# A decoder block on one core: the first MLP matrix multiplied with 512 columns instead of twice 256

## The chip, the cores and the metric

The kernel runs on one core of a Trainium2 chip. The metric is the device time of one execution in microseconds (us). Before the change three runs took 435.99, 436.06 and 436.56 us; their median is 436.06 us.

## The reference: what is computed

One decoder block for 256 tokens of width 1024, in float32: a gated mixer and block attention in parallel, an output projection, a squared-ReLU MLP, a gated embedding and a final norm. The change is in the MLP's first matrix:

```
x = x + merged @ w_out
h = rms_norm(x, norm_ffn_g)
x = x + square(relu(h @ w_ff1)) @ w_ff2      # w_ff1: 1024 x 4096, w_ff2: 4096 x 1024
```

The kernel multiplies the gained x without its norm factor and multiplies the squared result by the factor's square at the end.

## The kernel before

Each float32 operand of a matrix product is split into two parts that TensorE multiplies in one pass each: the high part (a rounded copy, made on ScalarE) and the low part (the rest, a subtraction on VectorE). A product is then the sum of three: high weights by high x, high weights by low x, low weights by high x. `mm3` (L116 to L119) issues these three for a block of 128 weight columns: 128 rows of weights against 256 columns (tokens).

Weights come as tiles of 1 MB in the order in which they are used (L34 to L45). A tile's load needs one of four raw buffers, its split (two pieces, each one ScalarE copy at L84 and one VectorE subtraction at L85) one of three pairs of split buffers. `weights` (L95) issues, on the engines' in-order queues, the splits up to two tiles ahead of the tile that it returns.

The MLP has 16 tiles of `w_ff1` and 16 of `w_ff2`. A tile of `w_ff1` gives 256 of the 4096 hidden features as two blocks f of 128 features, and each block takes eight steps k over the 1024 inputs: 16 triples of matmuls. Hidden features come in four groups b of four tiles j. The order on TensorE is: tiles (b=0, j=0) and (0,1) together (L556), which close 6 of 8 steps of all four blocks first and then the last two steps; tile (0,2); 16 transposes that bring x into token order (L584); tile (0,3); then tile (1,0), the first tile of `w_ff2` (24 matmuls of 512 columns, L125 to L128), tile (1,1), the next of `w_ff2`, and so on alternating.

A tile's result lies in one bank of PSUM, both blocks side by side (2 x 256 columns). Three banks rotate under the tag `mm` (L133); a matmul that starts a bank waits until the bank's last reader is done. After each tile `ff1_post` (L543) reads the bank once with a relu on ScalarE (L551), squares on VectorE (L553) and splits the square on ScalarE and VectorE (L107, L108). After tile (0,2) VectorE also copies the 16 transposes (L585, four copies), ScalarE squares them (L586, two), and the split of the first `w_ff2` tile stands behind these squares in ScalarE's queue; behind that stands the relu of tile (0,3).

Of the kernel before, what the change touches and what calls it, by code (L numbers as in the profile page):

```python
# [10 lines left out]
F32 = mybir.dt.float32  # L11
F32R = mybir.dt.float32r
AF = mybir.ActivationFunctionType
OP = mybir.AluOpType
AX = mybir.AxisListType

P = 128
S = 256
D = 1024
KD = D // P  # L20
# [3 lines left out]
CW = 256  # L24
# [26 lines left out]
def block_kernel(ctx: ExitStack, tc: tile.TileContext, xt, xk, pt, rows, wst, bsp, rel, buckets, wts, out):  # L51
    nc = tc.nc
    const = ctx.enter_context(tc.tile_pool(name="const", bufs=1))
    act = ctx.enter_context(tc.tile_pool(name="act", bufs=1))
    wpool = ctx.enter_context(tc.tile_pool(name="wpool", bufs=1))
    tmp = ctx.enter_context(tc.tile_pool(name="tmp", bufs=2))
# [30 lines left out]
    def split_to(n):  # L87
        while state["split"] < min(n, NTILE):
            i = state["split"]
            load_to(i + 4)  # L90
            split_tiles(i)
            for s in (slice(0, 1024), slice(1024, 2048)):
                split_piece(i, s)

    def weights(key, width, ahead=3):  # L95
        i = POS[key]
        split_to(i + ahead)
        k = 2048 // width
        return (hi[i].rearrange("p (k c) -> p k c", k=k), lo[i].rearrange("p (k c) -> p k c", k=k))


    def pair_tile(tag, name, k=KD):
        return act.tile([P, k, 2, S], F32R, tag=tag, name=name)

    def split_act(dst, src):

        nc.scalar.activation(dst[:, :, 0], src, AF.Copy)  # L107
        nc.vector.tensor_sub(dst[:, :, 1], src, dst[:, :, 0].bitcast(F32))  # L108
# [7 lines left out]
    def mm3(o, wh, wl, x, first, last, **kw):  # L116
        nc.tensor.matmul(o, wh, x[:, 0], start=first, stop=False, **kw)  # L117
        nc.tensor.matmul(o, wh, x[:, 1], start=False, stop=False, **kw)  # L118
        nc.tensor.matmul(o, wl, x[:, 0], start=False, stop=last, **kw)  # L119
# [13 lines left out]
    def bank(tag="mm", bufs=3, shape=(P, 2, 256)):  # L133
        return ps.tile(list(shape), F32, tag=tag, name=f"{tag}_t", bufs=bufs)
# [80 lines left out]
    def proj_T(key, x, mid=None, ahead=3):  # L215

        wh, wl = weights(key, CW, ahead)
        o = bank()
        for f in range(2):
            fs = slice(f * P, (f + 1) * P)  # L220
            for k in range(KD):
                mm3(o[:, f], wh[:, k, fs], wl[:, k, fs], x[:, k], k == 0, k == KD - 1)
            if f == 0 and mid:
                mid()
        return o
# [49 lines left out]


    sgu_a = act.tile([P, 2, D], F32, tag="kT", name="sgu_a")
    sgu_b = act.tile([P, 2, D], F32, tag="ln", name="sgu_b")
    wsT = sgu_a[:, 0].rearrange("p (g t) -> p g t", g=8)
    bsg = sgu_a[:, 1].rearrange("p (g t) -> p g t", g=8)  # L280
    ln_g, ln_b = sgu_b[:, 0], sgu_b[:, 1]

    def row_bcast(eng, dst, src):
        eng.dma_start(dst, bass.AP(tensor=src.tensor, offset=src.offset, ap=[[0, P], [1, D]]))
# [42 lines left out]
    o = proj_T(("w_in", 0), xg2)  # L327
# [4 lines left out]
    o = proj_T(("w_in", 1), xg2)  # L332
# [3 lines left out]
    o = proj_T(("w_in", 2), xg2)  # L336
    u_post(2, o)
    normalise_x(3)
    o = proj_T(("w_in", 3), xg2)
# [37 lines left out]
    for j in range(4):  # L377
        o = proj_T(("w_in", 8 + j), hT)
# [11 lines left out]
    sc_sb, pt_sb, yb = {}, {}, {}  # L390
# [91 lines left out]
    for J in range(2):  # L482
        a, b, c = 2 * J, 2 * J + 1, 4 * J
# [19 lines left out]
    xs1 = pair_tile("xA", "xs1")  # L503
# [10 lines left out]
    for i in range(3):  # L514
        wh, wl = weights(("w_out", i), 1024)
# [10 lines left out]
    wh, wl = weights(("w_out", 3), 1024, ahead=2)  # L526
# [13 lines left out]

    fs_ = {}

    def ff1_post(b, j, o):  # L543
        if j == 0:
            if b % 2 == 0:
                f8 = pair_tile("xB", f"fs{b}")
                fs_[b] = [f8[:, :4], f8[:, 4:]]
            else:
                fs_[b] = [pair_tile(tag, f"fs{b}{tag}", 4) for tag in ("qT", "kT")]
        r = tmp.tile([P, 2, S], F32, tag="th", name=f"r{b}_{j}", bufs=3)  # L550
        nc.scalar.activation(r, o, AF.Relu)  # L551
        q2 = tmp.tile([P, 2, S], F32, tag="sq", name=f"q{b}_{j}")
        nc.vector.tensor_mul(q2, r, r)  # L553
        split_act(fs_[b][j // 2][:, 2 * (j % 2):2 * (j % 2) + 2], q2)

    def ff1_pair():  # L556

        ws = [weights(("w_ff1", j), CW, ahead=3 - j) for j in range(2)]
        os_ = [bank(), bank()]
        for ks in (range(6), range(6, KD)):  # L560
            for j, (wh, wl) in enumerate(ws):
                for f in range(2):
                    fs = slice(f * P, (f + 1) * P)
                    for k in ks:
                        mm3(os_[j][:, f], wh[:, k, fs], wl[:, k, fs], xs1[:, k],
                            k == 0 and f == 0, k == KD - 1, skip_group_check=True)
        return os_


    late = act.tile([P, 4, D], F32, tag="TB", name="late")  # L570
# [7 lines left out]
    def x1_by_token():  # L578

        for t in range(2):  # L580
            for a in range(2):
                tb = ps_acc.tile([P, 512], F32, tag=f"acc{2 * t + a}", name=f"x1t{t}{a}")
                for k in range(4):
                    nc.tensor.transpose(tb[:, k * P:(k + 1) * P], xT[:, 4 * a + k, t * P:(t + 1) * P], ident)  # L584
                nc.vector.tensor_copy(x2[:, t, halves(a)], tb)  # L585
            nc.scalar.activation(scratch, x2[:, t], AF.Square, accum_out=ssq[:, 0, t:t + 1])  # L586
        m = small.tile([P, 2], F32, tag="ms", name="ms_x1")
        nc.vector.tensor_scalar(m, ssq[:, 0], 1.0 / D, EPS, op0=OP.mult, op1=OP.add)
        r = small.tile([P, 2], F32, tag="rr", name="rr_x1", bufs=1)
        nc.vector.reciprocal(r, m)  # L590
        return r

    for j, o in enumerate(ff1_pair()):
        ff1_post(0, j, o)
    ff1_post(0, 2, proj_T(("w_ff1", 2), xs1))
    rr1 = x1_by_token()
    ff1_post(0, 3, proj_T(("w_ff1", 3), xs1))
    row_bcast(nc.gpsimd, gfin, rows[2])
    nc.gpsimd.dma_start(pT, pt)
    split_act(pTs, pT)  # L600
# [3 lines left out]
    def ff2(b, j):  # L604
        wh, wl = weights(("w_ff2", 4 * b + j), 1024)
        for k in range(2):
            kk = 2 * j + k
            for c in range(2):
                tok3(acc[c], fs_[b][kk // 4][:, kk % 4], wh[:, k, halves(c)], wl[:, k, halves(c)],
                     b == 0 and kk == 0, False)  # L610

    for b in range(1, 4):
        for j in range(4):
            ff1_post(b, j, proj_T(("w_ff1", 4 * b + j), xs1))
            ff2(b - 1, j)
    for j in range(3):
        ff2(3, j)
# [58 lines left out]
    for i in range(2):  # L676
        wh, wl = weights(("w_ple_gate", i), 1024, ahead=3 - i)
# [136 lines left out]
```

## Time and profile before

| | |
|---|---|
| median of three runs | 436.06 us |
| the profiled execution | 436.34 us, of which the span of the trace is 434.5 us |
| TensorE busy | 424.8 us (98%) |
| VectorE busy | 268.7 us (62%) |
| ScalarE busy | 225.2 us (52%) |

The trace is of one execution. What lies outside the span is 1.84 us. In the rows further down, PE is TensorE, DVE is VectorE, ACT is ScalarE; times are from the start of the span. Matmuls are pipelined: the duration in a row is from the start of one to its end, while the next starts earlier; how fast the engine goes is read from the distance of the starts.

### The profile page before, as it was taken

Reading aid. Unit: us, or ns where it says so; the run is one execution under the profiler, and the core shown is the slowest. Engines: PE = TensorE matmul, PEld = TensorE weight load, DVE = VectorE, ACT = ScalarE, POOL = GpSimd, SP = SyncE. Lnnn points to the kernel's source line nnn. Section 1 sums busy time; section 2 is a strip of 40 time slices with the busy share of each in tenths; the row PEclk is TensorE's granted clock in tenths of the full one; section 3 lists DMA queues with packets and bytes.
Section 4 is the critical chain, followed back from the end, with each engine's and each line's share of the span. In section 5 each row is a group of like instructions: output and inputs, shape, how many; then the busy total and the mean of one; then the engine's idle time right before and its main releaser. Section 6 shows DMA issues by size and latency. Waiting matters only on the chain.

```text
span 434.5 us, 6951 instructions
## 1 busy us (share of the span) xinstructions
PE 424.8 (98%) x2908; PEld 389.5 (90%) x2908; DVE 268.7 (62%) x359; ACT 225.2 (52%) x351; POOL 13.0 (3%) x21
## 2 busy tenths in 40 slices
PE   8999999999999999999999999999999999999992
PEld 7789999988999989999999999999999999888882
DVE  3676889576765657745558765555555555546544
ACT  5685544266573656554355764444444444434824
POOL 1001020000000000000000000000000000000012
PEclk9999999999999999999999999999999999999997
DMA  8999549533525525455254475554555554552002
GB/s 271 424 385 380 191 160 388 212 117 134 202 66 181 194 99 195 145 195 195 97 195 151 164 288 198 193 193 186 179 185 179 171 189 181 190 198 89 2 2 97
DMA packets 13407, 81.02 MB, mean 186 GB/s; under 512 B 1509, under 2 KB 1781, under 8 KB 4800
## 3 DMA queue, kind: packets, MB, share of 16 engines
q1 hardware_dynamic: 12240, 77.34, 48.8%
q0 software_dynamic: 848, 2.96, 1.9%
q8 instruction: 23, 0.38, 0.4%
q10 hardware_dynamic: 288, 0.27, 0.2%
q14 instruction: 8, 0.07, 0.0%
HBM read 79.49 MB, written 1.07 MB: 185 GB/s over the span
## 4 chain that ended last, share of the span: by engine, by line
PE 90%; DMA 4%; ACT 2%; DVE 1%; issue 1%; POOL 0%; SPq 0%; POOLq 0%; ACTq 0%
PE mm_t L117 17%; PE mm_t L118 16%; PE mm_t L119 16%; PE y L125 7%; PE y L128 7%; PE y L127 7%; DMA raw<-wts 4%; PE acc L117 2%; PE mm_t L125 2%; PE acc L118 2%; PE acc L119 2%; PE mm_t L127 2%; PE mm_t L128 2%; PE mm_t L431 1%; PE sp L397 1%; PE yb_t L442 1%
## 5 line engine op out<-in xcount | busy, mean ns | idle before, releaser
L85 DVE TENSOR_TENSOR lo<-raw,hi 128x1024 fp32r<-128x1024 f32 (+1 forms) x140 | 162.7, 1206 | 62.0 <-ACT hi L84 62.0
L84 ACT ACTIVATE hi<-raw 128x1024 fp32r<-128x1024 f32 (+1 forms) x140 | 138.0, 1036 | 37.6 <-issue 25.1
L117 PE MATMUL mm_t<-hT,hi 128*128 128x256 f32 x256 | 74.4, 291 | 0.0
L117 PE MATMUL mm_t<-xs,hi 128*128 128x256 f32 x256 | 72.5, 283 | 0.0
L119 PE MATMUL mm_t<-xs,lo 128*128 128x256 f32 x256 | 72.4, 283 | 0.0
L118 PE MATMUL mm_t<-xs,hi 128*128 128x256 f32 x256 | 72.4, 283 | 0.0
L118 PE MATMUL mm_t<-hT,hi 128*128 128x256 f32 x256 | 72.3, 283 | 0.0
L119 PE MATMUL mm_t<-hT,lo 128*128 128x256 f32 x256 | 72.3, 283 | 0.0
L117 PEld LDWEIGHTS mm_t<-hT,hi 128*128 128x128 f32 x256 | 48.9, 191 | 2.6 <-issue 1.2
L118 PEld LDWEIGHTS mm_t<-xs,hi 128*128 128x128 f32 x256 | 49.1, 192 | 0.4
L117 PEld LDWEIGHTS mm_t<-xs,hi 128*128 128x128 f32 x256 | 49.1, 192 | 0.4
L119 PEld LDWEIGHTS mm_t<-xs,lo 128*128 128x128 f32 x256 | 49.1, 192 | 0.0
L118 PEld LDWEIGHTS mm_t<-hT,hi 128*128 128x128 f32 x256 | 49.0, 191 | 0.1
L119 PEld LDWEIGHTS mm_t<-hT,lo 128*128 128x128 f32 x256 | 48.9, 191 | 0.0
L551 ACT ACTIVATE r<-mm_t 128x512 f32<-128x512 f32 x16 | 9.5, 593 | 44.5 <-PE mm_t L119 44.5
L553 DVE TENSOR_TENSOR q<-r 128x512 f32<-128x512 f32 x16 | 11.0, 690 | 34.0 <-ACT r L551 34.0
L412 ACT ACTIVATE s<-s,nm 128x256 f32<-128x256 f32 (+1 forms) x32 | 14.2, 444 | 22.8 <-DVE nm L408 22.8
L128 PE MATMUL y<-hi,fs 128*128 128x512 f32 x64 | 24.9, 390 | 0.0
L127 PE MATMUL y<-lo,fs 128*128 128x512 f32 x64 | 24.9, 390 | 0.0
L125 PE MATMUL y<-hi,fs 128*128 128x512 f32 x64 | 19.8, 391 | 0.0
L117 PE MATMUL acc<-mT,hi 128*128 128x256 f32 x64 | 18.2, 285 | 0.0
L117 PE MATMUL mm_t<-xg,hi 128*128 128x256 f32 x64 | 18.2, 284 | 0.0
(195 smaller groups left out, 728.1 us busy)
## 6 DMA issues: line engine op xcount, KB each, us to landing
raw<-wts SPq DMA_DIRECT2D x67, 1024.0 KB, 4.9
TB<-rvd POOLq DMA_DIRECT2D x1, 2048.0 KB, 15.6
raw<-wts SPq DMA_DIRECT2D x4, 256.0 KB, 4.7
raw<-wts SPq DMA_DIRECT2D x2, 512.0 KB, 6.8
xtok<-xk SPq DMA_DIRECT2D x2, 512.0 KB, 10.3
sgu_b<-rows SPq DMA_DIRECT2D x2, 512.0 KB, 9.9
out<-ots SPq DMA_DIRECT2D x4, 256.0 KB, 2.0
xg<-xt SPq DMA_DIRECT2D x1, 512.0 KB, 7.4
```

The costliest lines, as they stand in the source:

```text
L84: nc.scalar.activation(hi[i][:, s], raw[i][:, s], AF.Copy)
L85: nc.vector.tensor_tensor(lo[i][:, s], raw[i][:, s], hi[i].bitcast(F32)[:, s], op=OP.subtract)
L117: nc.tensor.matmul(o, wh, x[:, 0], start=first, stop=False, **kw)
L118: nc.tensor.matmul(o, wh, x[:, 1], start=False, stop=False, **kw)
L119: nc.tensor.matmul(o, wl, x[:, 0], start=False, stop=last, **kw)
L125: nc.tensor.matmul(os_[t], x[:, 0, ts[t]], wh, start=first, stop=False)
L127: nc.tensor.matmul(os_[t], x[:, 0, ts[t]], wl, start=False, stop=False)
L128: nc.tensor.matmul(os_[t], x[:, 1, ts[t]], wh, start=False, stop=last)
L397: nc.tensor.matmul(sp[:, h, 0:256], qT[rs, c, P:2 * P], kT_[0][rs, c], start=True, stop=True)
L412: nc.scalar.activation(s[:, h, cs], s[:, h, cs], AF.Exp, bias=nm[:, i, h:h + 1], accum_out=sm[:, i, h:h + 1])
L551: nc.scalar.activation(r, o, AF.Relu)
L553: nc.vector.tensor_mul(q2, r, r)
```

## The change

The high weights are multiplied by both parts of x in one matmul of 512 columns (the high part's 256 and the low part's 256 lie side by side), so that a triple becomes a pair: one matmul of 512 columns that fills a whole bank, and one of 256 columns (low weights by high x) that adds to the bank's first half. The two halves of the bank have to be added. Each block f of a tile now has a bank of its own, two for a tile; ScalarE copies each to SBUF, VectorE adds the halves of both blocks (one operation), and one further VectorE operation does relu and square. The first two tiles use all three `mm` banks and the bank `yb`. The copies go to a buffer in the place of the two layer norm rows, which is cut in two.

```diff
-    sgu_b = act.tile([P, 2, D], F32, tag="ln", name="sgu_b")
+    ln_g, ln_b = [act.tile([P, D], F32, tag="ln", name=n, bufs=2) for n in ("ln_g", "ln_b")]
...
-    def ff1_post(b, j, o):
+    def ff1_mm(o, wh, wl, f, k):
+
+        fs = slice(f * P, (f + 1) * P)
+        nc.tensor.matmul(o, wh[:, k, fs], xs1[:, k], start=k == 0, stop=False, skip_group_check=True)
+        nc.tensor.matmul(o[:, 0], wl[:, k, fs], xs1[:, k, 0], start=False, stop=k == KD - 1, skip_group_check=True)
+
+    def ff1_copy(z, f, o):
+        nc.scalar.activation(z[:, f], o, AF.Copy)
+
+    def ff1_z(b, j):
+        return act.tile([P, 2, 2, S], F32, tag="ln", name=f"z{b}_{j}", bufs=2)
+
+    def ff1_tile(b, j):
+        wh, wl = weights(("w_ff1", 4 * b + j), CW)
+        z = ff1_z(b, j)
+        for f in range(2):
+            o = bank()
+            for k in range(KD):
+                ff1_mm(o, wh, wl, f, k)
+            ff1_copy(z, f, o)
+        ff1_post(b, j, z)
+
+    def ff1_post(b, j, z):
...
-        r = tmp.tile([P, 2, S], F32, tag="th", name=f"r{b}_{j}", bufs=3)
-        nc.scalar.activation(r, o, AF.Relu)
         q2 = tmp.tile([P, 2, S], F32, tag="sq", name=f"q{b}_{j}")
-        nc.vector.tensor_mul(q2, r, r)
+        nc.vector.tensor_add(z[:, :, 0], z[:, :, 0], z[:, :, 1])
+        nc.vector.scalar_tensor_tensor(q2, z[:, :, 0], 0.0, z[:, :, 0], op0=OP.max, op1=OP.mult)
         split_act(fs_[b][j // 2][:, 2 * (j % 2):2 * (j % 2) + 2], q2)
 
-    def ff1_pair():
+    def ff1_first():
 
         ws = [weights(("w_ff1", j), CW, ahead=3 - j) for j in range(2)]
-        os_ = [bank(), bank()]
+        os_ = [bank(), bank(), bank(), bank("yb", 1)]
...
+                        ff1_mm(os_[2 * j + f], wh, wl, f, k)
+        for j in range(2):
+            z = ff1_z(0, j)
+            for f in range(2):
+                ff1_copy(z, f, os_[2 * j + f])
+            ff1_post(0, j, z)
...
-            ff1_post(b, j, proj_T(("w_ff1", 4 * b + j), xs1))
+            ff1_tile(b, j)
             ff2(b - 1, j)
```

On ScalarE, from the split of tiles (0,3) and (1,0) to the reading of tile (0,3)'s result, the queue before reads so (hi and raw are weight tiles, r the relu of a result, fs the split square, x the token-order copy):

```order
L84 ACTIVATE hi_2413<-raw_2156 128x1024 [waits DMAHW1_49,Activation_49]
L84 ACTIVATE hi_2413<-raw_2156 128x1024
L84 ACTIVATE hi_2421<-raw_2284 128x1024 [waits DMAHW2_49,Activation_49]
L84 ACTIVATE hi_2421<-raw_2284 128x1024
L551 ACTIVATE r_2_2476<-mm_t 128x512 [waits PE_49]
L107 ACTIVATE fs_2398<-q_2_2478 128x2x256 [waits DVE_49]
L586 ACTIVATE late,ssq<-x_2282 128x1024 [waits DMASW3_49,DVE_49]
L586 ACTIVATE late,ssq<-x_2282 128x1024 [waits DVE_49,Activation_49]
L84 ACTIVATE hi_2514<-raw_2292 128x1024 [waits DMAHW3_49]
L84 ACTIVATE hi_2514<-raw_2292 128x1024
L551 ACTIVATE r_3_2569<-mm_t 128x512 [waits PE_49]
```

The same stretch of ScalarE's queue in the changed kernel, where z_2 and z_3 are the copies of tiles (0,2) and (0,3):

```order
L84 ACTIVATE hi_2388<-raw_2157 128x1024 [waits DMAHW1_49,Activation_49]
L84 ACTIVATE hi_2388<-raw_2157 128x1024
L84 ACTIVATE hi_2396<-raw_2285 128x1024 [waits DMAHW2_49,Activation_49]
L84 ACTIVATE hi_2396<-raw_2285 128x1024
L549 ACTIVATE z_2_2402<-mm_t 128x512 [waits PE_49,Activation_49]
L549 ACTIVATE z_2_2402<-mm_t 128x512 [waits PE_49]
L107 ACTIVATE fs_2372<-q_2_2439 128x2x256 [waits DVE_49]
L608 ACTIVATE late,ssq<-x_2283 128x1024 [waits DMASW3_49,DVE_49]
L608 ACTIVATE late,ssq<-x_2283 128x1024 [waits DVE_49,Activation_49]
L84 ACTIVATE hi_2476<-raw_2293 128x1024 [waits DMAHW3_49]
L84 ACTIVATE hi_2476<-raw_2293 128x1024
L549 ACTIVATE z_3_2482<-mm_t 128x512 [waits PE_49] x2
```

The one relu of a tile has become two copies; both copies of tile (0,3) stand where its relu stood, behind the two squares and the split of the first `w_ff2` tile.

On TensorE, at the step from block f=0 to block f=1 of tile (1,0), the queue before reads so (hi_2421 and lo_2422 are that tile's weights; both blocks write one bank):

```order
L117 MATMUL mm_t<-xs_2026,hi_2421 128x256
L118 MATMUL mm_t<-xs_2026,hi_2421 128x256
L119 MATMUL mm_t<-xs_2026,lo_2422 128x256
L117 MATMUL mm_t<-xs_2026,hi_2421 128x256
L118 MATMUL mm_t<-xs_2026,hi_2421 128x256
```

The same step of TensorE's queue in the changed kernel (hi_2396 and lo_2397 are the weights of tile (1,0)):

```order
L545 MATMUL mm_t<-xs_2027,hi_2396 128x512
L546 MATMUL mm_t<-xs_2027,lo_2397 128x256
L545 MATMUL mm_t<-xs_2027,hi_2396 128x512 [waits Activation_49]
L546 MATMUL mm_t<-xs_2027,lo_2397 128x256
L545 MATMUL mm_t<-xs_2027,hi_2396 128x512
```

The third row starts block f=1 in a bank of its own and has a wait for ScalarE that did not stand there.

On VectorE, from the low parts of tile (1,0)'s weights to the first copy of the transposes, the queue before reads so (q_2 is the square of tile (0,2)):

```order
L85 TENSOR_TENSOR lo_2422<-raw_2284,hi_2421 128x1024 [waits DMAHW2_49,PE_49,Activation_49]
L85 TENSOR_TENSOR lo_2422<-raw_2284,hi_2421 128x1024 [waits Activation_49]
L553 TENSOR_TENSOR q_2_2478<-r_2_2476 128x512 [waits Activation_49]
L108 TENSOR_TENSOR fs_2398<-q_2_2478,fs_2398 128x2x256 [waits Activation_49]
L585 COPY x_2282<-x1t_2482 128x512 [waits PE_49]
```

The same stretch of VectorE's queue in the changed kernel:

```order
L85 TENSOR_TENSOR lo_2397<-raw_2285,hi_2396 128x1024 [waits DMAHW2_49,PE_49,Activation_49]
L85 TENSOR_TENSOR lo_2397<-raw_2285,hi_2396 128x1024 [waits Activation_49]
L572 TENSOR_TENSOR z_2_2402<-z_2_2402 128x2x256 [waits Activation_49]
L573 SCALAR_TENSOR_TENSOR q_2_2439<-z_2_2402 128x512 [waits DVE_49]
L108 TENSOR_TENSOR fs_2372<-q_2_2439,fs_2372 128x2x256 [waits Activation_49]
L607 COPY x_2283<-x1t_2444 128x512 [waits PE_49]
```

The addition is one more VectorE operation in each tile, ahead of the square and of the copies of the transposes.

## Rows read from the trace of the kernel before

**Rows 1.** The page: TensorE's busy time; the chain that ended last by engine.
```profile
PE 424.8 (98%) x2908; PEld 389.5 (90%) x2908; DVE 268.7 (62%) x359; ACT 225.2 (52%) x351; POOL 13.0 (3%) x21
...
PE 90%; DMA 4%; ACT 2%; DVE 1%; issue 1%; POOL 0%; SPq 0%; POOLq 0%; ACTq 0%
```

**Rows 2.** TensorE's waits over the whole span: total, times, longest (us).
```profile
PE yb_t L179 <- DVE mhalf L139: 1.1, 1, 1.1
PE yb_t L272 <- DVE dg L266: 0.4, 1, 0.4
```

**Rows 3.** Timeline of TensorE in the MLP: start, duration (us), line, operation, tiles, count.
```profile
215.64 0.28 PE L117 MATMUL mm_t<-xs,hi 128*128 128x256 f32 x1
...
232.92 1.91 PE L584 MATMUL x1t<-ident,xg 128*128 128x128 f32 x16
234.59 0.36 PE L117 MATMUL mm_t<-xs,hi 128*128 128x256 f32 x1
...
243.29 0.28 PE L117 MATMUL mm_t<-xs,hi 128*128 128x256 f32 x1
...
246.17 0.63 PE L125 MATMUL y<-hi,fs 128*128 128x512 f32 x2
...
251.64 0.28 PE L117 MATMUL mm_t<-xs,hi 128*128 128x256 f32 x1
...
257.39 0.63 PE L125 MATMUL y<-hi,fs 128*128 128x512 f32 x2
```

**Rows 4.** Groups by line, one of the triple's: count, busy us, mean ns, idle.
```profile
L117 PE MATMUL mm_t<-xs,hi 128*128 128x256 f32 x256 | 72.5, 283 | 0.0
```

**Rows 5.** Timeline of ScalarE, 225 to 260 us.
```profile
225.92 0.60 ACT L551 ACTIVATE r<-mm_t 128x512 f32<-128x512 f32 x1 [4.65 <-PE mm_t L119]
227.28 0.63 ACT L107 ACTIVATE fs<-q 128x512 fp32r<-128x512 f32 x1 [0.76 <-DVE q L553]
227.81 0.58 ACT L551 ACTIVATE r<-mm_t 128x512 f32<-128x512 f32 x1
...
229.81 3.89 ACT L84 ACTIVATE hi<-raw 128x1024 fp32r<-128x1024 f32 x4
...
241.05 1.99 ACT L84 ACTIVATE hi<-raw 128x1024 fp32r<-128x1024 f32 x2
242.95 0.58 ACT L551 ACTIVATE r<-mm_t 128x512 f32<-128x512 f32 x1
...
257.59 0.60 ACT L551 ACTIVATE r<-mm_t 128x512 f32<-128x512 f32 x1 [2.91 <-PE mm_t L119]
```

**Rows 6.** Timeline of VectorE: two merge operations, then two tiles' low parts and (0,2)'s square.
```profile
196.33 0.68 DVE L453 SCALAR_TENSOR_TENSOR tb<-tb,yb_t 128x512 f32<-128x512 f32 x1
197.05 0.69 DVE L455 TENSOR_TENSOR ta<-ta,tb 128x512 f32<-128x512 f32 x1
...
230.89 4.63 DVE L85 TENSOR_TENSOR lo<-raw,hi 128x1024 fp32r<-128x1024 f32 x4 [0.26 <-ACT hi L84]
235.44 0.68 DVE L553 TENSOR_TENSOR q<-r 128x512 f32<-128x512 f32 x1
```

**Rows 7.** The page's DMA issues: count, KB each, median us from issue to landing.
```profile
raw<-wts SPq DMA_DIRECT2D x67, 1024.0 KB, 4.9
```

**Rows 8.** The last matmul; then windows: length, PE, PEld, DVE, ACT, POOL busy, PEclk, DMA.
```profile
426.08 0.28 PE L674 MATMUL g_last<-hi,xs 128*128 128x256 f32 x1
...
428.80:429.00 0.20, 0.00 (x0) 0.00 (x0) 0.14 (x1) 0.20 (x1) 0.00 (x0) 1.00 0.00 0
...
429.20:429.40 0.20, 0.00 (x0) 0.00 (x0) 0.14 (x1) 0.20 (x2) 0.00 (x0) 0.50 0.00 0
```

**Rows 9.** Timeline of TensorE at the start of the program.
```profile
1.12 4.96 PE L179 MATMUL yb_t<-ones 128*128 128x128 f32 x22 [1.12 <-DVE mhalf L139]
...
7.04 0.40 PE L128 MATMUL vo<-hi,xg 128*128 128x512 f32 x1
7.27 0.39 PE L127 MATMUL vo<-lo,xg 128*128 128x512 f32 x1
```

More of the change, by code (lines that the diff above doesn't have):

```diff
@@ L277, in block_kernel @@
     sgu_a = act.tile([P, 2, D], F32, tag="kT", name="sgu_a")
-    sgu_b = act.tile([P, 2, D], F32, tag="ln", name="sgu_b")
+    ln_g, ln_b = [act.tile([P, D], F32, tag="ln", name=n, bufs=2) for n in ("ln_g", "ln_b")]
     wsT = sgu_a[:, 0].rearrange("p (g t) -> p g t", g=8)
     bsg = sgu_a[:, 1].rearrange("p (g t) -> p g t", g=8)
-    ln_g, ln_b = sgu_b[:, 0], sgu_b[:, 1]
     def row_bcast(eng, dst, src):
@@ L562, in ff1_pair @@
                 for f in range(2):
-                    fs = slice(f * P, (f + 1) * P)
                     for k in ks:
-                        mm3(os_[j][:, f], wh[:, k, fs], wl[:, k, fs], xs1[:, k],
-                            k == 0 and f == 0, k == KD - 1, skip_group_check=True)
-        return os_
+                        ff1_mm(os_[2 * j + f], wh, wl, f, k)
[4 more added lines that the diff above has]
+            ff1_post(0, j, z)
     late = act.tile([P, 4, D], F32, tag="TB", name="late")
@@ L591, in x1_by_token @@
         return r
-    for j, o in enumerate(ff1_pair()):
-        ff1_post(0, j, o)
-    ff1_post(0, 2, proj_T(("w_ff1", 2), xs1))
+    ff1_first()
+    ff1_tile(0, 2)
     rr1 = x1_by_token()
-    ff1_post(0, 3, proj_T(("w_ff1", 3), xs1))
+    ff1_tile(0, 3)
     row_bcast(nc.gpsimd, gfin, rows[2])
```

## The prediction

> **What bounds the kernel now.** I read the page's busy shares and its chain first. TensorE is busy 424.8 of 434.5 us, and 90% of the chain that ended last is TensorE's [rows 1]. The table of waits says the same from the other side: over the whole span TensorE waited 1.1 us for VectorE once and 0.4 us once, both long before the MLP [rows 2]. So in the MLP every column that TensorE doesn't multiply is time won, as long as nothing makes it wait.
>
> How fast it goes there is in its timeline [rows 3]. A tile of `w_ff1` between two tiles of `w_ff2` runs from 251.64 to 257.39: 48 matmuls of 256 columns in 5.75 us, 119.8 ns each. A tile of `w_ff2` runs from 246.17 to 251.64: 24 matmuls of 512 columns in 5.47 us, 227.9 ns each. Twice the columns cost less than twice the time; that difference is all that the change can win on TensorE.
>
> **What the change removes.** A triple of 256, 256 and 256 takes 3 x 119.8 = 359.4 ns; the pair of 512 and 256 takes 227.9 + 119.8 = 347.7 ns, 11.7 ns less. There are 256 triples (one of the triple's three lines, each x256) [rows 4], so TensorE gets 3.0 us. Ends for this term: no row shows the two sizes in turn on this path, so nothing at all may be saved; the upper end is 256 x (2 x 0.120 - 0.2267) = 3.4 us, with the 0.23 us that lies between 512-column starts at its least (7.04 to 7.27 in [rows 9] is of that size). I take 3.0, from the whole tiles.
>
> The rows show a fixed cost of about 12 ns in a matmul: 119.8 against 227.9 for double the columns [rows 3]. The Trainium skill, TensorE: Matmul & The Clock Gate, section Back-to-back issue gap, gives columns divided by 2.4 GHz plus 2.5 ns; by that estimate a triple saves 2.5 ns, all of them 0.6 us, the end would be 2.0 above the median instead of 0.3 with the wait worked out below, and it speaks against this change. The trace disagrees (119.8 ns where the page has 109), and the measurement decides.
>
> **What it adds, per tile.** ScalarE: two copies of 512 elements for one relu, one more at about 0.59 us (0.58 and 0.60) [rows 5]. VectorE: one more operation, 0.69 us, and 0.72 us when the next needs its result (196.33 to 197.05) [rows 6]; the operation with relu and square has the form of the row at 196.33 (0.68). In the alternating part this is hidden: a tile of each kind takes 11.2 us, both queues work on splits for two tiles ahead, and ScalarE still waits 2.91 us for TensorE before the relu at 257.59 [rows 5]. Without that cover it would be 0.7 us a tile. The later low parts also release the raw buffers later, by at most 2.2 us (below); a load takes 4.9 us [rows 7] and its tile is split two tiles (11 us) later, so SP's queue passes nothing on.
>
> **The new wait.** Before the alternation there is no cover. I follow the queues of ScalarE and VectorE there, as they are written out with the change. Two facts meet. Each tile now takes two of three banks, so block f=1 of tile (1,0) needs the bank that held block f=0 of tile (0,3) (the blocks take in turn banks 1, 2, 3 and `yb`, then 1, 2 for (0,2), 3, 1 for (0,3), 2, 3 for (1,0)). And the copy that frees it stands on ScalarE behind tile (0,2)'s chain, the squares and the first `w_ff2` split. When does it come?
>
> - The pair starts at 215.64 [rows 3]. Tile (0,0) closes after 28 triples; before that was 225.72, and the relu started at 225.92 [rows 5], 0.20 later. Now 28 x 0.3477 gives 225.37, so the copy of its second block starts at 225.57 and ends at 226.17.
> - VectorE adds and squares to 227.58 (0.72 + 0.69); ScalarE splits at 227.62. The next copies follow 0.53 us apart, as 227.28 to 227.81 [rows 5]: at 228.15 and 228.70, to 229.28. Addition and square to 230.72, split at 230.75, and the splits of tiles (0,3) and (1,0) at 231.29 instead of 229.81 [rows 5]: 1.48 later.
> - VectorE's low parts follow by 1.48. Tile (0,2)'s addition stands at 236.92 where its square stood at 235.44 [rows 6], and its extra 0.72 moves all behind it by 2.20: transposes' copies, squares, the `w_ff2` split from 241.05 to 243.25, and the place of tile (0,3)'s relu from 242.95 [rows 5] to 245.15. There the copy runs, to about 245.75.
> - TensorE, 72 triples of 11.7 ns ahead by then, arrives at block f=1 at 243.29 [rows 3] - 0.84 = 242.45. It stands until about 245.78: 3.3 us.
>
> Its first low part is there for tile (0,3): 230.89 + 1.48 + 1.2 = 233.6, against 234.59 - 0.56 = 234.0. Behind the waiting matmul stand eight pairs and the `w_ff2` tile, which is split by then; nobody else waits for them. After it no bank is late: the copy that frees the next one stands behind one more split, by the same count at about 251.7, and TensorE asks for it at 245.78 + 2.78 + 5.47 + 2.78 = 256.8.
>
> **Sum.** TensorE starts block f=1 at 245.78 instead of 243.29: 2.5 later. The 184 triples that remain give back 184 x 11.7 ns = 2.15 us. The profiled execution, 436.34 us (434.5 span and 1.84 around it), becomes 436.7; the median of the runs, 436.06, lies 0.28 lower, so 436.4 there. The gain of 3.0 us is gone into a wait of 3.3 us. Its own range is 435.6 to 437.0 (saving up to 3.4, chain 0.3 either way).
>
> **The clock on top of it.** After the last matmul, which starts at 426.08 and ends 0.28 later, the granted clock still reads 1.00 until 429.00 and 0.50 from 429.20 [rows 8]: about 2.7 us after TensorE stopped it fell from 2.4 to 1.2 GHz. The new pause is longer than that. So the eight pairs after it and some of the next tile may run at half speed. The same skill page, section Why this matters for your kernels, names idle stretches between matmul bursts as what brings the slow clock back; the end of this trace agrees, and no run here shows it in the middle of a program. What would it cost? At the start 22 matmuls of 128 columns take 4.96 us, 225 ns each [rows 9], where 16 of that shape later take 1.67 us, 104 ns each (232.92 to 234.59) [rows 3]; full pace is there by 7.04. That stretch prints a clock of 1.00, yet the pace is half: up to 5.9 us at half pace, up to 2.9 us lost. Ends: 0 and 2.9. I take 1.5, the middle, since the pause outlasts the 2.7 us only just, and the row of the start is of an engine that had long been idle.
>
> **Rivals and chances.** A difference under 0.2%, 0.87 us, can't be told from none here.
> - Forecast, 0.45: the wait and the slow clock: 436.4 + 1.5 = 437.9, range 437.0 to 439.3.
> - The wait alone, 0.34: 436.4. For it: in the rows the clock needed most of such a pause to fall, and a pause 0.6 us shorter could leave it.
> - No wait, or one under 1.5 us, 0.14: the whole gain stays, 436.06 - 3.0 = 433.1, with half of it 434.6. For it: TensorE never waits in the MLP now [rows 2]. Against it: the copy can't overtake the squares and the split in ScalarE's queue.
> - The pair saves nothing (the 512 columns take what two matmuls took, or a cost of the change of sizes eats it), 0.07: TensorE arrives at 243.29, waits 2.5 us, and gives nothing back: 438.6, slower without any help of the clock.
>
> Faster: 0.14. Within 0.2%: the wait alone but for a little, 0.33. Slower: the rest, 0.53. The range takes in the forecast, the wait alone, and the half gain's near side: 435.2 to 439.2.
>
> **What the profile after will show.** A wait of TensorE for ScalarE's L549 in the table of waits, once, 3 to 3.5 us, ending near 245.8; the splits of ScalarE at 231.3 and 243.3; starts 348 ns apart from pair to pair; the granted clock at 0.50 for some us from 245 on, with pairs at twice the distance. A second wait in the alternating part would prove the cover there wrong; tiles of 5.56 us and no wait at all would prove the forecast wrong, and a wait at a clock of 1.00 throughout leaves the second case.

## The result, and the profile after

The changed kernel takes 439.51 us (median of seven runs, 437.44 to 440.59), the kernel before 436.01 beside it; the ratio over all runs is 1.0068, 95% interval 1.0051 to 1.0084. It is slower by 0.7%. The forecast was 437.9 us with a range to 439.2: the side and the mechanism are right, the size is 1.6 us short, and the median stands 0.3 us above the range's end.

The profiled execution took 440.59 us, one of the longest, with a span of 438.8 us. The page of the kernel after, TensorE's busy time, granted clock in 40 slices, and the chain by engine, which answer to [rows 1]:

```profile
PE 426.0 (97%) x2652; PEld 378.1 (86%) x2652; DVE 280.2 (64%) x375; ACT 234.3 (53%) x367; POOL 13.0 (3%) x21
...
PEclk9999999999999999999999699999999999999997
...
PE 87%; DMA 4%; DVE 3%; ACT 2%; issue 1%; POOL 0%; SPq 0%; POOLq 0%; ACTq 0%
```

There are 256 matmuls fewer, and yet TensorE is busy for longer. One slice of the clock has a 6 (the 7 at the end lies behind the last matmul). TensorE's waits of the kernel after (us in total, times, longest), which answer to [rows 2]:

```profile
PE mm_t L545 <- ACT z L549: 3.1, 1, 3.1
PE yb_t L179 <- DVE mhalf L139: 1.1, 1, 1.1
PE yb_t L272 <- DVE dg L266: 0.4, 1, 0.4
```

One new wait, for a copy of ScalarE. Its place in TensorE's timeline of the kernel after (start, duration), which answers to [rows 3]:

```profile
242.66 0.28 PE L546 MATMUL mm_t<-xs,lo 128*128 128x256 f32 x1
246.02 0.80 PE L545 MATMUL mm_t<-xs,hi 128*128 128x512 f32 x1 [3.08 <-ACT z L549]
246.62 0.41 PE L546 MATMUL mm_t<-xs,lo 128*128 128x256 f32 x1
246.83 0.63 PE L545 MATMUL mm_t<-xs,hi 128*128 128x512 f32 x1
...
251.31 0.98 PE L125 MATMUL y<-hi,fs 128*128 128x512 f32 x2
...
257.15 0.39 PE L545 MATMUL mm_t<-xs,hi 128*128 128x512 f32 x1
...
262.79 0.63 PE L125 MATMUL y<-hi,fs 128*128 128x512 f32 x2
```

Block f=1 of tile (1,0) starts at 246.02 (243.29 before). Its eight pairs run to 251.31, 5.29 us, where a later tile needs 5.64 us for all sixteen (257.15 to 262.79). ScalarE's timeline of the kernel after shows what the wait was for; it answers to [rows 5]:

```profile
225.13 1.30 ACT L549 ACTIVATE z<-mm_t 128x512 f32<-128x512 f32 x2 [3.83 <-PE mm_t L546]
...
231.53 3.89 ACT L84 ACTIVATE hi<-raw 128x1024 fp32r<-128x1024 f32 x4
...
243.50 1.99 ACT L84 ACTIVATE hi<-raw 128x1024 fp32r<-128x1024 f32 x2
245.39 1.06 ACT L549 ACTIVATE z<-mm_t 128x512 f32<-128x512 f32 x2
```

The splits stand at 231.53 and 243.50 (229.81 and 241.05 before), the copy that frees the bank at 245.39. The windows around the wait (length; PE, PEld, DVE, ACT, POOL busy; granted clock; DMA share; GB/s):

```profile
242.80:245.00 2.20, 0.14 (x2) 0.00 (x0) 0.76 (x3) 2.20 (x4) 0.55 (x1) 1.00 0.00 0
245.00:246.00 1.00, 0.00 (x0) 0.00 (x0) 1.00 (x2) 1.00 (x3) 0.00 (x0) 0.62 0.67 197
246.00:248.00 2.00, 1.98 (x6) 1.69 (x7) 1.97 (x3) 0.45 (x1) 0.00 (x0) 0.50 0.42 74
...
250.00:252.00 2.00, 2.00 (x8) 1.71 (x7) 1.82 (x3) 2.00 (x4) 0.00 (x0) 0.50 0.58 246
252.00:254.00 2.00, 2.00 (x10) 1.59 (x10) 1.97 (x3) 0.30 (x1) 0.00 (x0) 0.98 0.28 33
```

A mean of 0.62 from 245 to 246 puts the fall to 1.2 GHz at 245.24, 2.3 us after the last matmul ended (242.94); 0.98 from 252 to 254 puts the return at about 252.1. So TensorE worked some 6 us at half pace after it had started again.

The account of this execution, against the span before (434.5 to 438.8, 4.3 us more): restart 246.02 - 243.29 = +2.73; the eight pairs of block f=1, 5.29 instead of 2.88: +2.41; the first `w_ff2` tile, 5.84 instead of 5.47 us (251.31 to 257.15): +0.37; eleven later tiles, 5.64 instead of 5.75: -1.21. Sum +4.30.

The seven runs lie in groups: 437.44 and 437.65; 439.07 to 439.58; 440.52 and 440.59. The profile is one of the last. That the groups differ in how long the clock stayed low fits their mean granted clocks (0.996, 0.992 to 0.993, 0.986), but it is argued: only the longest run has a trace, and the middle group's clock hardly stands apart from the kernel before, whose runs read 0.993 to 0.997.

### The profile page after: what moved, and what is told of

The parts are those of the page before. It is cut to its first block, busy times and chain, and to the rows that moved or that the text cites. A ratio compares the mean times of both kernels' runs of the same rounds, so it can differ in the third digit from the quotient of the medians.

```text
span 438.8 us, 6470 instructions
## 1 busy us (share of the span) xinstructions
PE 426.0 (97%) x2652; PEld 378.1 (86%) x2652; DVE 280.2 (64%) x375; ACT 234.3 (53%) x367; POOL 13.0 (3%) x21
## 4 chain that ended last, share of the span: by engine, by line
PE 87%; DMA 4%; DVE 3%; ACT 2%; issue 1%; POOL 0%; SPq 0%; POOLq 0%; ACTq 0%
PE mm_t L545 12%; PE mm_t L117 9%; PE mm_t L118 9%; PE mm_t L119 9%; PE y L125 7%; PE y L128 7%; PE y L127 7%; PE mm_t L546 6%; DMA raw<-wts 4%; PE acc L117 2%; PE mm_t L125 2%; PE acc L119 2%; PE acc L118 2%; PE mm_t L127 2%; PE mm_t L128 2%; DVE lo L85 1%
## 5 line engine op out<-in xcount | busy, mean ns | idle before, releaser
L545 PE MATMUL mm_t<-xs,hi 128*128 128x512 f32 x248 | 90.6, 406 | 3.1 <-ACT z L549 3.1
L546 PE MATMUL mm_t<-xs,lo 128*128 128x256 f32 x248 | 70.7, 285 | 0.0
L545 PEld LDWEIGHTS mm_t<-xs,hi 128*128 128x128 f32 x248 | 47.7, 192 | 15.0 <-ACT z L549 3.4
L546 PEld LDWEIGHTS mm_t<-xs,lo 128*128 128x128 f32 x248 | 48.0, 194 | 0.4
L549 ACT ACTIVATE z<-mm_t 128x512 f32<-128x512 f32 x31 | 18.1, 593 | 36.5 <-PE mm_t L546 36.4
L572 DVE TENSOR_TENSOR z<-z 128x512 f32<-128x512 f32 x16 | 11.1, 692 | 33.8 <-ACT z L549 33.8
L117 PE MATMUL mm_t<-xg,hi 128*128 128x256 f32 x64 | 18.2, 284 | 0.0
L118 PE MATMUL mm_t<-xg,hi 128*128 128x256 f32 x64 | 18.1, 283 | 0.0
L119 PE MATMUL mm_t<-xg,lo 128*128 128x256 f32 x64 | 18.1, 283 | 0.0
```

The lines of the kernel that those rows point to most:

```text
L545: nc.tensor.matmul(o, wh[:, k, fs], xs1[:, k], start=k == 0, stop=False, skip_group_check=True)
L546: nc.tensor.matmul(o[:, 0], wl[:, k, fs], xs1[:, k, 0], start=False, stop=k == KD - 1, skip_group_check=True)
L549: nc.scalar.activation(z[:, f], o, AF.Copy)
```

## The experiments

My theory: the loss is the bank's wait, its length set by the copy's place in ScalarE's queue, and on top the clock that falls in it. Rivals: the alternating part has lost its cover; the pair saves nothing; the slow stretch is not the pause's.

**A free bank.** Block f=0 of tile (0,3) takes `yb`, so that three blocks later a bank is free:

```diff
-            o = bank()
+            o = bank("yb", 1) if (b, j, f) == (0, 3, 0) else bank()
```

> The changed kernel with one edit: block f=0 of tile (0,3) goes to the bank yb, which is free since 229.5 us, so that block f=1 of tile (1,0) finds a bank free and no wait for the copy is left. Theory (the wait and the clock that falls in it are the whole loss): no wait of TensorE for L549, clock 1.00 throughout, tiles of w_ff1 at 5.64 us; 11 to 15 tiles at 0.11 us less than before make about 1.7 us, less up to 0.5 us for the first w_ff2 tile's split, which now comes just in time: 434.3 to 434.9 us. Rival (the alternating part has lost its cover: one more ScalarE and one more VectorE operation a tile show there): several short waits in the alternation and no better than 436 us. Rival (the pair itself costs as much as the triple): 436.0.

Measured: 434.87 us (434.73 to 435.35) beside 436.22, ratio 0.997 (0.9958 to 0.9981). Its wait of TensorE in the MLP, and the start of the first `w_ff2` tile in its timeline:

```profile
PE mm_t L546 <- DVE lo L85: 0.3, 1, 0.3
```

```profile
245.70 0.28 PE L546 MATMUL mm_t<-xs,lo 128*128 128x256 f32 x1
245.81 0.63 PE L125 MATMUL y<-hi,fs 128*128 128x512 f32 x2
```

The wait for L549 is gone, and the `w_ff2` tile follows at once. One bank turns 0.7% slower into 0.3% faster. The wait of 0.3 us that is left stands in the tile of `w_ff1` behind it, tile (1,1). Its first rows on TensorE, then VectorE's low parts for it, here and in the kernel before:

```profile
251.30 0.39 PE L545 MATMUL mm_t<-xs,hi 128*128 128x512 f32 x1
251.94 0.39 PE L546 MATMUL mm_t<-xs,lo 128*128 128x256 f32 x1 [0.26 <-DVE lo L85]
```

```profile
250.66 2.36 DVE L85 TENSOR_TENSOR lo<-raw,hi 128x1024 fp32r<-128x1024 f32 x2 [0.18 <-ACT hi L84]
```

```profile
247.26 2.36 DVE L85 TENSOR_TENSOR lo<-raw,hi 128x1024 fp32r<-128x1024 f32 x2 [0.17 <-ACT hi L84]
```

VectorE is 3.4 us later there: 0.4 since the MLP starts later in this execution, and by the prediction's count 2.9 from the added operations (2.2, and 0.72 for one more tile). The tile takes 6.16 us (251.30 to 257.46); the ten tiles of `w_ff1` behind it take 5.64, with no wait. So the rival with the lost cover falls for the alternating part, but at its entrance the added work costs 0.5 us.

**The wait filled.** TensorE multiplies ones into a bank that nobody reads, instead of standing:

```diff
+            if (b, j, f) == (1, 0, 1):
+                fill = bank("yb", 1)
+                for i in range(14):
+                    nc.tensor.matmul(fill[:, 0, :P], ones, ones, start=True, stop=True)
             o = bank()
```

> The changed kernel with 14 float32 matmuls of ones (128 columns, into the free bank yb, read by nobody) ahead of the matmul that waits: TensorE works through the 3.1 us instead of standing. Theory (bank wait plus fallen clock): the place of the restart stays at 246.0 us, since ScalarE's chain sets it, but the clock stays at 1.00; so every run at 437.3 to 437.7 us, where the runs of the changed kernel spread from 437.4 to 440.6. Rival (the slow stretch after the pause is something else than the pause: loads or VectorE's reads against TensorE's): half pace after 246 us and 439 to 440.6 us as in the changed kernel.

Measured: 437.70 us, all seven runs from 437.37 to 437.83, ratio 1.0031 (1.0019 to 1.0042). TensorE's timeline (a float32 matmul of ones has two rows) and a window behind it:

```profile
242.43 3.29 PE L561 MATMUL yb_t<-ones 128*128 128x128 f32 x28
245.66 0.50 PE L545 MATMUL mm_t<-xs,hi 128*128 128x512 f32 x1
246.00 0.28 PE L546 MATMUL mm_t<-xs,lo 128*128 128x256 f32 x1
```

```profile
246.00:250.00 4.00, 4.00 (x23) 3.42 (x22) 3.17 (x5) 2.16 (x5) 0.00 (x0) 1.00 0.59 188
```

The block starts no earlier than ScalarE's chain lets it (245.66; the copy starts at 245.04 and takes 0.58), the clock stays at 1.00, and the spread of 3.15 us has become 0.46. The wait alone is worth about 1.5 us against the kernel before. What the changed kernel takes above 437.7 comes with the pause; in its profiled execution it is the clock, and for its other runs that is argued from the spread.

**The pair cut in two.** The 512 columns as two matmuls of 256, all else as changed:

```diff
-        nc.tensor.matmul(o, wh[:, k, fs], xs1[:, k], start=k == 0, stop=False, skip_group_check=True)
+        for h in range(2):
+            nc.tensor.matmul(o[:, h], wh[:, k, fs], xs1[:, k, h], start=k == 0 and h == 0, stop=False,
+                             skip_group_check=True)
```

> The changed kernel with the 512-column matmul cut in two of 256 columns into the two halves of the same bank; copies, additions and banks as in the changed kernel. It prices the pair alone. Theory: tiles of w_ff1 at 5.75 us as before the change, the wait about 2.7 us (arrival 0.5 later), restart near 246.2; 436.0 + 2.9 = 438.9 us where the clock holds and up to 442 where it falls. Rival (the pair saves nothing): tiles at 5.64 us and the same time as the changed kernel, 437.4 to 440.6.

Measured: 440.69 us (440.49 to 440.84), ratio 1.0099 (1.0085 to 1.0113). Its wait and its place:

```profile
PE mm_t L546 <- ACT z L551: 2.7, 1, 2.7
```

```profile
243.05 0.28 PE L548 MATMUL mm_t<-xs,lo 128*128 128x256 f32 x1
245.99 0.50 PE L546 MATMUL mm_t<-xs,hi 128*128 128x256 f32 x2 [2.66 <-ACT z L551]
```

TensorE arrives later, restarts at the same time, and its tiles take 5.75 us as before the change. So the pair saves 0.11 us a tile, 6.9 ns a triple (0.11 us in 16), and the restart is ScalarE's. Here too the clock fell, but behind the restart, as a window shows:

```profile
246.00:247.00 1.00, 1.00 (x8) 1.00 (x9) 1.00 (x2) 0.42 (x1) 0.00 (x0) 0.91 0.22 86
```

A mean of 0.91 puts the fall at 246.82, 0.8 us after TensorE had started again. Block f=1 takes 4.47 us (245.99 to 250.46) instead of 2.88: these 1.6 us are most of the 1.8 that the time has above the 438.9 that I gave for a clock that holds.

**All of one size first.** On top of the free bank, a block multiplies its eight steps with 512 columns and then its eight with 256:

```diff
+        for k in ks:
+            nc.tensor.matmul(o, wh[:, k, fs], xs1[:, k], start=k == 0, stop=False, skip_group_check=True)
+        for k in ks:
+            nc.tensor.matmul(o[:, 0], wl[:, k, fs], xs1[:, k, 0], start=False, stop=k == KD - 1, skip_group_check=True)
```

> e1_free_bank with the order inside a block changed: first all matmuls of 512 columns (8 steps k), then all of 256. It asks why the pair takes 352 ns (0.2333 + 0.12) where 512 columns alone take 227.9 ns in w_ff2's tiles. Theory A (the turn from 256 to 512 columns costs the 5 to 6 ns): 512-column starts 0.227 to 0.228 us apart, tiles of 5.56 us, 0.08 us a tile less than e1_free_bank, 1.2 us less in all: 433.2 to 433.8 us. Theory B (it is the operands, weights as the stationary and both parts of x as the moving one): 0.233 still, tiles of 5.64 us and the time of e1_free_bank within 0.3 us.

Measured: 434.35 us (434.00 to 434.86), ratio 0.9956 (0.9943 to 0.9968). Tiles in the alternating part take 5.56 us, so theory B falls, and there the turn between the sizes costs 5 ns a pair. One such tile, from its first matmul to the next tile's:

```profile
263.17 1.98 PE L546 MATMUL mm_t<-xs,hi 128*128 128x512 f32 x8
...
268.73 0.63 PE L125 MATMUL y<-hi,fs 128*128 128x512 f32 x2
```

It is not a cost of every turn. With the free bank, sizes in turn, tile (0,2) ahead of the alternating part took 5.55 us, 347 ns a pair:

```profile
227.22 0.39 PE L545 MATMUL mm_t<-xs,hi 128*128 128x512 f32 x1
...
232.77 1.91 PE L606 MATMUL x1t<-ident,xg 128*128 128x128 f32 x16
```

The same tile took 5.55 or 5.56 in the traces of two more variants with that order (the filled wait, the copy ahead of the split), and 5.65 in the trace of the changed kernel and of the wait filled in part. These kernels have the same matmuls up to there, so it goes by the execution; what decides is open.

The total fell by 0.5 us, not by 1.2. Grouping also hid the late low parts of tile (1,1) (5.56 instead of 6.16 us), but the first two tiles together took 11.95 us instead of 11.2. Their first matmuls show why:

```profile
216.04 1.09 PE L546 MATMUL mm_t<-xs,hi 128*128 128x512 f32 x4
217.38 0.90 PE L546 MATMUL mm_t<-xs,hi 128*128 128x512 f32 x2 [0.24 <-DVE xs L114]
218.11 0.88 PE L548 MATMUL mm_t<-xs,lo 128*128 128x256 f32 x6
```

The first six of 512 columns take 2.07 us, where the next block's six take 1.40 (218.83 to 220.23): taken one behind the other, they come to each part of x before VectorE has made it. Of these 0.67 us only 0.24 shows as a wait.

**The first two tiles step by step again**, the other 14 as in the last kernel:

```diff
-                    ff1_mm(os_[2 * j + f], wh, wl, f, ks)
+                    for k in ks:
+                        ff1_mm(os_[2 * j + f], wh, wl, f, (k,))
```

> e4_grouped with the first two tiles taken step by step again, as in the changed kernel (512, 256, 512, 256), since their grouped order waited 0.2 us for the low parts of x; the other 14 tiles stay grouped. Theory: no wait for x, tiles of 5.56 us from tile (0,2) on, 0.0 to 0.3 us less than e4_grouped: 434.0 to 434.4 us. Rival (the wait was covered by a later one): the same as e4_grouped, 434.3.

Measured: 433.55 us (433.46 to 433.76), ratio 0.9936 (0.9923 to 0.9950): the fastest version, 0.6% below the kernel before. It gained more than I expected; the grouped first tiles cost 0.8 us, not 0.3: I had counted the wait that is shown and not the distance of the starts. A block in its timeline:

```profile
261.94 1.98 PE L546 MATMUL mm_t<-xs,hi 128*128 128x512 f32 x8
263.75 0.99 PE L548 MATMUL mm_t<-xs,lo 128*128 128x256 f32 x7
```

Eight matmuls of 512 columns start within 1.81 us, 226 ns each.

**The copy ahead of the split.** The changed kernel's banks, one move in ScalarE's queue:

```diff
-        wh, wl = weights(("w_ff1", 4 * b + j), CW)
+        late_split = (b, j) == (0, 3)
+        wh, wl = weights(("w_ff1", 4 * b + j), CW, ahead=2 if late_split else 3)
...
             ff1_copy(z, f, o)
+            if late_split and f == 0:
+                split_to(POS["w_ff1", 3] + 3)
```

> The changed kernel, its banks untouched, with one move in ScalarE's queue: the split of the first w_ff2 tile is issued behind the first copy of tile (0,3), not ahead of both. Theory (the place of the copy in the queue sets the length of the wait): the copy runs at 243.5 instead of 245.4, TensorE waits 1.2 to 1.4 us instead of 3.1, the clock stays at 1.00 in so short a pause, the w_ff2 tile's split is still in time: 437.5 - 1.9 = 435.5 to 435.8 us. Rival (the bank alone decides, the copy waits for something else): wait of 3.1 us and 437.4 to 440.6.

Measured: 435.81 us (eleven runs, 435.50 to 436.30), ratio 0.9989 (0.9980 to 0.9997). Its wait, and ScalarE's timeline:

```profile
PE mm_t L545 <- ACT z L549: 1.2, 1, 1.2
```

```profile
243.05 0.58 ACT L549 ACTIVATE z<-mm_t 128x512 f32<-128x512 f32 x1
243.53 2.00 ACT L84 ACTIVATE hi<-raw 128x1024 fp32r<-128x1024 f32 x2
```

The split's 1.9 us left the wait. The clock reads 1.00 behind it in the trace, and the eleven times lie within 0.8 us, so nothing shows a fall in the others.

**A part of the wait filled**, 5 matmuls of ones instead of 14:

```diff
-                for i in range(14):
+                for i in range(5):
```

> e2_wait_filled with 5 instead of 14 matmuls of ones: TensorE works for 1.1 us of the wait and then stands for about 2.0 us. It asks whether the slow stretch hangs on the length of the pause. Theory: 2.0 us is shorter than the 2.7 us after which the clock fell at the end of the kernel before, so the clock holds in all runs: 437.4 to 437.8 us, as with the whole wait filled. Rival (any pause of some length lets it fall in part of the runs): a spread up to 440 us.

Measured: 437.81 us, but two of five runs at 438.93 and three from 437.54 to 437.81; ratio 1.0042 (1.0028 to 1.0055). The profiled execution, one of the three, waits

```profile
PE mm_t L545 <- ACT z L549: 1.8, 1, 1.8
```

with a clock of 1.00 behind it. My expectation fell: a pause well under the 2.7 us at the end of the program adds 1.1 us in a part of the runs. That this is the clock is argued from the spread (with the whole wait filled there is hardly any) and from the mean granted clocks, 0.989 and 0.992 in the two slower runs and 0.993 to 0.996 in the others; neither of the two has a trace. The pair cut in two shows that the clock can fall after TensorE has started again, so that a pause ends sooner does not by itself keep it up.

## Why the prediction was right or wrong

- **What bounds the kernel: right.** TensorE waited nowhere in the MLP, and what was taken off its columns counted as soon as nothing stood in the way (the free bank).
- **The new wait: right,** by place, releaser, number and length. Forecast: arrival 242.45, release 245.78, 3.3 us. Measured: 242.78 (0.12 behind the last start), 246.02, 3.24 us. The chain came out 0.24 late, since the first pair itself closed later. Cutting either half of the reason cut the wait: another bank took it away, the split behind the copy left 1.2 us.
- **What a pair saves: wrong, the term that failed.** I summed 227.9 + 119.8 ns from two places where each size runs by itself and got 11.7 ns a triple; no row showed the sizes in turn, and I had named nothing as the lower end, yet took the sum. In turn they take 352.5 ns in the alternating part (5.64 us in 16), so 6.9 ns are saved: a cost of the change of sizes, which my last rival had eating all of the saving (0.07), ate 0.4 of it. After the wait that gives back 11.5 x 0.11 = 1.27 us, not 2.15. Grouped, the sum's 347.5 ns come back (5.56 us in 16); in tile (0,2) the sum held in turn too in three traces, so why the turn costs something later is not shown. By the formula of the Trainium skill, TensorE: Matmul & The Clock Gate, section Back-to-back issue gap, a triple would by estimate save 2.5 ns; both orders saved more (6.9 and 11.9).
- **The wait alone: a size off.** 436.06 + 2.73 - 1.27 = 437.5 instead of my 436.4, and the two fastest runs (437.44, 437.65) and the filled wait (437.70) are there. So the wait alone was already outside 0.2%, and that rival's chance should have been part of slower. Its range of 435.6 to 437.0 took in a larger saving and no smaller one; from the ends that it names it comes to 435.8 to 436.7.
- **The clock: right in kind, too small.** In the trace it fell in the pause, as I gave it the larger chance. Of the ends 0 and 2.9 I took the middle, 1.5; the runs show 0 to 3.1 above 437.5, and 2.0 for the median. The row of the start was the better guide than I allowed: 6 us at half pace here, 5.9 there [rows 9]. No run stands at that middle: 437.9 lies in a gap between the groups, and nothing here forecasts which group a run falls in.
- **The rest of the sum.** 437.9 to 439.5 is 0.9 from the pair, 0.2 from the chain, 0.5 from the clock.
- **The hidden work: right for this kernel.** ScalarE's and VectorE's added operations, the later loads and the cut buffer showed nowhere in the alternating part: tiles of 5.75 us with the pair cut in two, as before, and no second wait. That holds because TensorE itself was 2.7 us late; with the free bank, where it wasn't, tile (1,1) lost 0.5 us to the later low parts.

## What to carry to other kernels

When a change gives a result two buffers where it had one, go through the turns of the buffers by hand where the work doesn't alternate, and look at what stands ahead of the releasing copy in its engine's queue: here three microseconds of other engines' work, hidden until then, landed on TensorE, and one idle bank undid it. A saving summed from two shapes that run apart has to be taken with doubt where they will run in turn; running all of one shape first got it back where the operands were ready, and lost 0.7 us where they were still being made. A wait of TensorE costs more than its length when the clock falls in it or behind it, and not in every run: a new spread between runs of one program is a sign of it.

## What the runs showed of the hardware

- In the changed kernel's trace the clock fell to 1.2 GHz 2.3 us after the last matmul in the middle of the program, and was back only 6 us after TensorE had started again, at 252.1; that cost 2.5 + 0.4 us (eight pairs in 5.29 us that take 2.82 at full pace, and the next tile). With the same 3.2 us filled with matmuls of ones it stayed at 2.4 GHz in the trace, and seven runs lie within 0.46 us.
- The fall can come behind the pause: after 2.7 us without a matmul (the pair cut in two) the clock fell 0.8 us after TensorE had started again, and that cost 1.6 us.
- A pause of 1.2 us left the times within 0.8 us of each other in eleven runs; with one of about 1.8 us two of five runs took 1.1 us longer.
- In the alternating tiles a matmul of 512 columns takes 226 ns from start to start behind another of its size and about 233 ns in turn with one of 256 (352.5 - 119.8). In tile (0,2) of three traces it took 227 in turn (347 - 120).
